# A scan written level by level between the tiles of four projections

## The chip, the cores and the metric

One core of one Trainium2 chip runs the whole kernel in one launch. The metric is the device time of the launch in microseconds (us), as a median over runs. The engines are named as the profile names them: PE is TensorE's matmul side and PEld its weight load, DVE is VectorE, ACT is ScalarE, POOL is GpSimd, SP is SyncE, which here only issues DMAs.

## The reference

One layer of a decoder trunk on 1024 tokens of width 1024, all in float32: a combined input projection, three mixers, an output projection with layer norm, and a mixture of experts. The change touches the input projection and the third mixer, a gated linear recurrence (HGRN2) with 4 heads of 64x64 state:

```
h = x @ w_in                     # 2840 columns, split into gu, gv, nq, ..., hq, hf, hi, hg
def hgrn2_mixer(q, f_logit, i, lower_bound):
    log_f = logaddexp(log(lb), log1p(-lb) + log_sigmoid(f_logit))
    k = (1 - lb) * sigmoid(-f_logit)
    def step(S, inp):            # chunk after chunk, S is the 64x64 state of a head
        b = cumsum(lfc, axis=2)
        decay = exp(where(causal, b[t] - b[s], -inf))
        attn = einsum('bhtd,bhsd,bhtsd->bhts', qc, kc, decay)
        o = attn @ ic + (qc * exp(b)) @ S
        S = exp(b_last) * S + (kc * exp(b_last - b)).T @ ic
    ...
y_a = gmlp_mixer(gelu(gu), gelu(gv), ...)     # first mixer: takes gu and gv
y   = head_rms_norm(concat(y_a, y_b, y_c)) ; y_c part * silu(hg)
```

Here `i` is the column group hi ("the values"), `q` is hq, `f_logit` is hf, and hg is the output gate. hi is needed where `attn` meets `ic`, in its diagonal part, and in the state's update; hg, gv and gu are not needed in the recurrence at all.

## The kernel before

**Stages.** `phase1` loads x, turns it, makes all projections, the recurrence and the gMLP mixer; `phase2` does the attention mixer and the output projection; `moe` the experts. In the profiled run the first stage covers about the first 335 us.

**Projections.** A float32 product is made of three single-pass products of a high and a low part (`mm3`, L78: lines L83, L84, L85 are its three matmuls). `load_w` (L136) fetches 256 columns of w_in in four DMAs on SP (L144), makes the high part on ACT (L72) and the low part on POOL (L76). The weight tiles are two in turn, so a load waits until the projection before the last is through with its tile. `token_major(w, c)` (L199) makes 128 tokens by 256 columns: 24 matmuls into one PSUM tile `pj`. `feature_major` (L149) makes 128 columns by 512 tokens. `pj` has three buffers. "A tile" below is one `token_major` call with the copy that takes its result out of PSUM; hi, hg, gv and gu have eight each (c = 0 to 7), 32 in all.

**The recurrence.** `hgrn` (L489) is called four times, for a pair of heads j and a half hh of the sequence: (0,0), (0,1), (1,0), (1,1). A call has three parts. The front (L499 to L537) makes gates, the running sum b (L510, DVE) and `dgs`, the diagonal of attn; L537, on POOL, starts the result yc as hi times dgs. Then come seven levels (LEVELS = 64 to 1) that build the matrix A by halving: POOL subtracts (L548), ACT takes two exponentials (L549, L550), DVE multiplies three times (L551 into `kq`, L554 twice into `qq`; both double buffered), PE makes 8 matmul records (L557) into `lv`, and DVE copies the level into A under a mask (L558). Last, for four chunks in turn, PE multiplies A by hi (L569) and the state by q (L572), DVE adds to yc (L573), PE makes the state's update (L576) and DVE applies it (L580). A has a single buffer; POOL clears it (L540).

**The order.** The program is not run in the order in which it is written. The compiler (L1596, `schedule_with_timeline_sim=True`) lays out each engine's queue ahead of time on a modelled timeline: of the instructions that are ready there, the one written first goes first. On the chip each queue then keeps that order. Written order is therefore a priority. Before the change it is: features of hf, features of hq, all eight tiles of hi (copied out by DVE, L241), the four calls of `hgrn`, the eight tiles of hg (copied out by ACT, L247), those of gv and gu (ACT, L251), and then the columns of the attention mixer.

Of the kernel before, what the change touches and what calls it, by code (L numbers as in the profile page):

```python
# [10 lines left out]
AF = mybir.ActivationFunctionType  # L11
OP = mybir.AluOpType
# [7 lines left out]
NT = 8  # L20
# [31 lines left out]
class Trunk:  # L52
# [71 lines left out]
    def phase1(self, ctx_nsa, ctx_q, x1d, acc):  # L124
# [60 lines left out]
        with ExitStack() as ctx:  # L185
# [13 lines left out]
            def token_major(w, c):  # L199
                wh, wl, n = w  # L200
                pj = ps.tile([128, 512], F32, name="pj", bufs=3)
                sl = slice(c % 4 * 128, c % 4 * 128 + 128)
                self.mm3(pj[:, :n], KD, lambda k: [xs[c // 4][p][:, k, sl] for p in range(2)], lambda k: [w[p][:, k, 0:n] for p in range(2)])
                return pj
# [19 lines left out]
            with ExitStack() as c2:  # L224
                hp = self.pool(c2, "hgw")
                self.hgrn_consts(hp)
                fl, hq = {}, {}
                for j in range(2):
                    for hh in range(2):
                        pj = feature_major(w, 128 * j, hh)  # L230
                        fl[j, hh] = hp.tile([128, 512], F32, name="fl", bufs=2)
                        nc.scalar.activation(fl[j, hh], pj, AF.Copy)
                w = load_w((C_HQ, 256))
                for j in range(2):
                    for hh in range(2):
                        pj = feature_major(w, 128 * j, hh)
                        hq[j, hh] = hp.tile([128, 512], F32, name="hq", bufs=4)
                        nc.scalar.activation(hq[j, hh], pj, AF.Copy)
                w = load_w((C_HI, 256))
                for c in range(NT):  # L240
                    nc.vector.tensor_copy(hi[:, c], token_major(w, c)[:, :256])  # L241
                for j in range(2):
                    for hh in range(2):
                        self.hgrn(hp, fl[j, hh], hq[j, hh], hi, yc, j, hh)
                w = load_w((C_HG, 256))
                for c in range(NT):
                    nc.scalar.activation(hgt[:, c], token_major(w, c)[:, :256], AF.Copy)  # L247
                for c0, dst in ((C_GV, gv), (C_GU, gu)):
                    w = load_w((c0, 256))
                    for c in range(NT):  # L250
                        nc.scalar.activation(dst[:, c], token_major(w, c)[:, :256], AF.Copy)  # L251

            ns = self.pool(self.ctx, "nsa", side="right")
            self.gate = ns.tile([128, NT, 24], F32, name="gate")
# [231 lines left out]
            nc.gpsimd.memset(t, 0.0)  # L486
        self.nlev = 0

    def hgrn(self, hp, fl, hq, hi, yc, j, hh):  # L489

        nc, ps = self.nc, self.ps
        W = 512
        tmp = lambda: hp.tile([128, W], F32, name="tmp", bufs=4)
        chunk = lambda t: t.rearrange("p (c t) -> p c t", t=128)
        k = hp.tile([128, W], F32, name="k", bufs=2)
        b = hp.tile([128, W], F32, name="b", bufs=2)

        t1, t2, t3 = tmp(), tmp(), tmp()
        nc.scalar.activation(t1, fl, AF.Abs)  # L499
        nc.scalar.activation(t1, t1, AF.Exp, scale=-1.0)  # L500
        nc.scalar.activation(t1, t1, AF.Ln, bias=1.0)
        nc.vector.tensor_scalar(t2, fl, -60.0, None, OP.max)
        nc.scalar.activation(t2, t2, AF.Exp, scale=-1.0)
        nc.scalar.activation(t2, t2, AF.Ln, bias=1.0, scale=self.lb[:, j:j + 1])
        nc.vector.scalar_tensor_tensor(t1, fl, 0.0, t1, OP.min, OP.subtract)
        nc.gpsimd.tensor_tensor(k, t1, fl, OP.subtract)
        nc.scalar.activation(k, k, AF.Exp)
        nc.gpsimd.tensor_scalar(k, k, self.oml[:, j:j + 1], None, OP.mult)
        nc.gpsimd.tensor_tensor(t1, t1, t2, OP.add)
        nc.vector.tensor_tensor_scan(b, self.rs, t1, 0.0, OP.mult, OP.add)  # L510
        bc = chunk(b)

        qe = hp.tile([128, W], F32, name="qe", bufs=2)
        nc.scalar.activation(qe, b, AF.Exp)
        ebl = hp.tile([128, 4], F32, name="ebl", bufs=2)
        nc.vector.tensor_copy(ebl, chunk(qe)[:, :, 127])
        nc.vector.tensor_tensor(qe, qe, hq, OP.mult)
        nc.gpsimd.tensor_tensor(chunk(t3), bc[:, :, 127:128].to_broadcast([128, 4, 128]), bc, OP.subtract)
        nc.scalar.activation(t3, t3, AF.Exp)
        nc.vector.tensor_tensor(t3, t3, k, OP.mult)  # L520
        kt = hp.tile([128, 4, 128], F32, name="kt", bufs=2)
        pt = ps.tile([128, 4, 128], F32, name="lv", bufs=3)
        for u in range(4):
            nc.tensor.transpose(pt[:, u], t3[:, u * 128:(u + 1) * 128], self.ident)
        nc.scalar.activation(kt, pt, AF.Copy)

        t4 = tmp()
        nc.gpsimd.tensor_tensor(t4, hq, k, OP.mult)
        dg = ps.tile([128, 4, 2], F32, name="o", bufs=2)
        for u in range(4):  # L530
            nc.tensor.matmul(dg[:, u], t4[:, u * 128:(u + 1) * 128], self.hs, start=True, stop=True)
        dgs = hp.tile([128, 4, 2], F32, name="dgs", bufs=2)
        nc.vector.tensor_copy(dgs, dg)
        hij = hi[:, 4 * hh:4 * hh + 4, j * 128:(j + 1) * 128]
        ycj = yc[:, 4 * hh:4 * hh + 4, j * 128:(j + 1) * 128]
        heads = lambda t: t.rearrange("p c (e d) -> p c e d", d=64)
        nc.gpsimd.tensor_tensor(heads(ycj), heads(hij), dgs[:, :, :, None].to_broadcast([128, 4, 2, 64]), OP.mult)  # L537

        A = hp.tile([128, 4, 2, 128], F32, name="A", bufs=1)
        nc.gpsimd.memset(A, 0.0)  # L540
        for l, h in enumerate(LEVELS):
            w = 2 * h
            kb, qb = self.kq[self.nlev % 2], self.qq[self.nlev % 2]
            self.nlev += 1
            dd = tmp()
            seg = lambda t: t.rearrange("p (s w) -> p s w", w=w)
            bs, ds, qs, ks, kbs = seg(b), seg(dd), seg(hq), seg(k), seg(kb)
            nc.gpsimd.tensor_tensor(ds, bs, bs[:, :, h - 1:h].to_broadcast([128, W // w, w]), OP.subtract)  # L548
            nc.scalar.activation(ds[:, :, 0:h], ds[:, :, 0:h], AF.Exp, scale=-1.0)  # L549
            nc.scalar.activation(ds[:, :, h:w], ds[:, :, h:w], AF.Exp)  # L550
            nc.vector.tensor_tensor(kbs[:, :, 0:h], ks[:, :, 0:h], ds[:, :, 0:h], OP.mult)  # L551
            for e in range(2):
                r = slice(64 * e, 64 * e + 64)
                nc.vector.tensor_tensor(qb[r, e].rearrange("p c (g h) -> p (c g) h", h=h), qs[r, :, h:w], ds[r, :, h:w], OP.mult)  # L554
            lv = ps.tile([128, 4, 2, 64], F32, name="lv", bufs=3)
            for u in range(4):
                nc.tensor.matmul(lv[:, u], kb[:, u * 128:(u + 1) * 128], qb[:, :, u, :], start=True, stop=True)  # L557
            nc.vector.copy_predicated(  # L558
                A.rearrange("p c e (g two h) -> p (c e) g two h", two=2, h=h)[:, :, :, 1, :],
                self.lmi[:, None, l, :].to_broadcast([128, 8, 64]).rearrange("p u (g h) -> p u g h", h=h),  # L560
                lv.rearrange("p u e (g h) -> p (u e) g h", h=h))

        for u in range(4):
            c = 4 * hh + u
            sl = slice(u * 128, (u + 1) * 128)
            o = ps.tile([128, 128], F32, name="o", bufs=2)
            Sc, Sn = self.S[j][c % 2], self.S[j][(c + 1) % 2]
            for e in range(2):
                nc.tensor.matmul(o[:, e * 64:e * 64 + 64], A[:, u, e, :], hij[:, u, e * 64:e * 64 + 64],  # L569
                                 start=(c == 0 or e == 0), stop=(c == 0))  # L570
            if c:
                nc.tensor.matmul(o, qe[:, sl], Sc, start=False, stop=True)  # L572
            nc.vector.tensor_tensor(ycj[:, u], ycj[:, u], o, OP.add)  # L573
            if c < NT - 1:
                su = ps.tile([128, 128], F32, name="o", bufs=2)
                nc.tensor.matmul(su, kt[:, u], hij[:, u], start=True, stop=True)  # L576
                for e in range(2):
                    r = slice(64 * e, 64 * e + 64)
                    if c:
                        nc.vector.scalar_tensor_tensor(Sn[r, r], Sc[r, r], ebl[r, u:u + 1], su[r, r], OP.mult, OP.add)  # L580
                    else:
                        nc.vector.tensor_copy(Sn[r, r], su[r, r])
# [1017 lines left out]
```

## Time and profile before

| | us |
|---|---|
| median of the runs shown | 1260.39 |
| lowest run | 1260.23 |
| the profiled execution: time | 1260.82 |
| the profiled execution: span of its instructions | 1259.1 |
| PE busy in the span | 1152.3 (92%) |
| DVE busy | 838.4 (67%) |
| ACT busy | 682.1 (54%) |
| POOL busy | 486.7 (39%) |
| mean granted clock of TensorE | 0.963 |

Times in the trace count from the first instruction of the span. The profiled execution takes 1.7 us more than its span, and it lies 0.4 us over the median. A busy share is a mean over stages with different limits, so the rows further down are all cut to a stretch of time: 61.5 to 225 us holds the eight tiles of hi, the scan and the tiles of hg, gv and gu.

### The profile page before, as it was taken

What the parts mean: (1) busy time and instruction counts of PE and PEld (TensorE: products, weight loads), DVE (VectorE), ACT (ScalarE), POOL (GpSimd) and SP (SyncE); (2) the same over time, 40 slices, a digit from 0 to 9 for tenths busy, and PEclk for the clock granted to TensorE, in tenths of its full rate; (3) what the DMA queues carried; (4) which work ended last, traced back from release to release, by engine and by line L of the source; (5) the groups of instructions that cost most, each with busy time, mean ns of one, the idle gap of its engine ahead of it and who ended that gap; (6) DMA issues with size and microseconds to landing.
All of it is one profiled execution on the core that took longest, in us unless ns stands there. A gap on an engine that the chain in (4) does not pass through costs nothing. (4 is left out here: it accounts for less than half of the span.)

```text
span 1259.1 us, 18585 instructions
## 1 busy us (share of the span) xinstructions
PE 1152.3 (92%) x6413; PEld 976.5 (78%) x6413; DVE 838.4 (67%) x1473; ACT 682.1 (54%) x1310; POOL 486.7 (39%) x530
## 2 busy tenths in 40 slices
PE   8998789999897999998898999889999999999992
PEld 6898789888786777787777777668888878888871
DVE  4238876654336778778787876648675875856677
ACT  5416473432436557547474643447575775665672
POOL 6535853563236455433434344112130320311144
PEclk9999899999899999999999899889999999999997
DMA  6120101655135122102111006759887997979782
GB/s 220 42 51 18 34 2 34 178 159 152 49 117 172 38 93 76 68 26 68 42 52 42 35 1 240 250 140 324 309 275 251 302 388 247 329 249 337 240 281 116
DMA packets 92913, 190.41 MB, mean 151 GB/s; under 512 B 15964, under 2 KB 50812, under 8 KB 92784
## 3 DMA queue, kind: packets, MB, share of 16 engines
q1 hardware_dynamic: 81984, 161.97, 38.1%
q0 software_dynamic: 8208, 21.59, 7.5%
q10 hardware_dynamic: 2592, 5.25, 1.1%
q8 instruction: 67, 1.10, 0.4%
q14 instruction: 62, 0.51, 0.1%
HBM read 163.15 MB, written 32.06 MB: 155 GB/s over the span
## 5 line engine op out<-in xcount | busy, mean ns | idle before, releaser
L49 DVE TENSOR_TENSOR wl<-raw,wh 128x1024 fp32r<-128x1024 f32 x192 | 226.5, 1220 | 46.7 <-ACT wh L49 46.4
L49 ACT ACTIVATE wh<-raw 128x1024 fp32r<-128x1024 f32 x192 | 189.7, 1051 | 5.2 <-PE T L49 2.7
L685 POOL TENSOR_SCALAR p<-p,co 128x640 f32<-128x640 f32 (+7 forms) x128 | 89.6, 719 | 97.8 <-DVE co L678 87.2
L727 ACT ACTIVATE p<-S,nm 128x640 f32<-128x640 f32 (+7 forms) x128 | 89.6, 708 | 30.4 <-DVE nm L718 13.7
L72 ACT ACTIVATE th<-T 128x512 fp32r<-128x512 f32 (+1 forms) x148 | 81.4, 580 | 41.0 <-PE T L749 39.1
L76 DVE TENSOR_TENSOR tl<-T,th 128x512 fp32r<-128x512 f32 (+1 forms) x148 | 94.3, 652 | 7.5 <-ACT th L72 6.8
L83 PE MATMUL pj<-wh,xh 128*128 128x256 f32 (+1 forms) x320 | 94.0, 294 | 2.2 <-DVE gate L311 2.2
L84 PE MATMUL pj<-wl,xh 128*128 128x256 f32 (+1 forms) x320 | 94.1, 294 | 0.0
L85 PE MATMUL pj<-wh,xl 128*128 128x256 f32 (+1 forms) x320 | 93.8, 293 | 0.0
L76 POOL TENSOR_TENSOR wl<-wraw,wh 128x512 fp32r<-128x512 f32 (+1 forms) x44 | 61.5, 1410 | 78.9 <-ACT wh L72 78.6
L49 POOL DMA_INDIRECT acc<-yv,idx x21 | 38.9, 1855 | 132.2 <-ACT yv L49 122.8
L49 PE MATMUL u<-wh,xth 128*128 128x256 f32 (+1 forms) x256 | 86.9, 340 | 0.0
L749 PE MATMUL T<-ident,p 128*128 128x128 f32 x528 | 85.4, 287 | 1.0 <-DVE ks L168 1.0
L718 DVE TENSOR_REDUCE nm<-S 128x1 f32<-128x640 f32 (+7 forms) x96 | 85.1, 886 | 1.5
L49 PE MATMUL u<-wh,xtl 128*128 128x256 f32 (+1 forms) x256 | 84.9, 332 | 0.0
L49 PE MATMUL u<-wl,xth 128*128 128x256 f32 (+1 forms) x256 | 84.8, 331 | 0.0
L752 PE MATMUL O<-tl,v 128*128 128x512 f32 x132 | 63.1, 478 | 19.0 <-DVE tl L76 18.3
L49 PE MATMUL y<-wh,hth 128*128 128x512 f32 x184 | 76.6, 416 | 4.2 <-ACT hth L49 3.5
L712 PE MATMUL S<-ks,q 128*128 128x512 f32 (+3 forms) x192 | 70.1, 368 | 11.0 <-ACT pc L696 7.7
L749 PEld LDWEIGHTS T<-ident,p 128*128 128x128 f32 x528 | 69.1, 149 | 13.1 <-issue 2.5
L49 PE MATMUL g<-wh,xth 128*128 128x512 f32 x184 | 74.5, 405 | 1.7 <-ACT xth L49 1.7
L49 PE MATMUL g<-wh,xtl 128*128 128x512 f32 x184 | 74.5, 405 | 0.0
(411 smaller groups left out, 3210.0 us busy)
## 6 DMA issues: line engine op xcount, KB each, us to landing
raw<-in_exp_w_gate_dram SPq DMA_DIRECT2D x64, 512.0 KB, 4.5
raw<-in_exp_w_up_dram SPq DMA_DIRECT2D x64, 512.0 KB, 8.6
raw<-in_exp_w_down_dram SPq DMA_DIRECT2D x64, 512.0 KB, 10.3
wraw<-in_w_in_dram SPq DMA_DIRECT2D x36, 256.0 KB, 2.7
q<-qd SPq DMA_DIRECT2D x64, 128.0 KB, 3.9
xr<-in_x_dram SPq DMA_DIRECT2D x8, 512.0 KB
x<-in_x_dram SPq DMA_DIRECT2D x8, 512.0 KB, 4.1
raw<-acc SPq DMA_DIRECT2D x8, 512.0 KB, 7.6
```

The source lines that it names most:

```text
L49: return lambda *a, **k: self.tc.keep_in_program_order(getattr(self.engine, name)(*a, **k))
L72: A.activation(hi, src, AF.Copy)
L76: (G if eng == "g" else V).tensor_tensor(lo, src, f(hi), OP.subtract)
L83: nc.tensor.matmul(ps, lh, rh, start=(k == 0), stop=False)
L84: nc.tensor.matmul(ps, lh, rl, start=False, stop=False)
L85: nc.tensor.matmul(ps, ll, rh, start=False, stop=(k == n - 1))
L685: nc.gpsimd.tensor_scalar(P[b][h], P[b][h], co[:, b, h:h + 1], 0.0, OP.mult, OP.add)
L712: nc.tensor.matmul(reg, hd(0, h0 + u), ks, start=True, stop=False)
L718: nc.vector.tensor_reduce(nm[:, 1 + br, h0:h0 + per], S.rearrange("p (u k) -> p u k", u=per)[:, :, 0:n], axis=AX, op=OP.max, negate=True)
L727: nc.scalar.activation(P[1 + br][h], S[:, 512 * u:512 * u + n], AF.Exp, bias=nm[:, 1 + br, h:h + 1], accum_out=sums[:, 1 + br, h:h + 1])
L749: nc.tensor.transpose(Tp[:, h], P[b][h][:, kb * 128:kb * 128 + 128], self.ident)
L752: nc.tensor.matmul(O, v, t, start=(n == 0 and t is th), stop=(n == len(jobs) - 1 and t is tl))
```

## The change

Three things. The four projections hi, hg, gv and gu become one generator, `projections`, that yields after each tile; all 32 results are copied out by ACT, where hi's eight were copied out by DVE. `hgrn` takes one tile after each level, and in the call (0,0) one more behind the seventh level, so that all of hi is written before A first meets it: 8 + 7 + 7 + 7 tiles, and the last three of gu behind the scan. Since `load_w` stands inside the generator, a weight load is written where the first tile of its projection is asked for. And L537 (yc = hi times dgs, POOL) moves from ahead of the levels to behind them. No tile, buffer or matmul is added or removed.

```diff
-                w = load_w((C_HI, 256))
-                for c in range(NT):
-                    nc.vector.tensor_copy(hi[:, c], token_major(w, c)[:, :256])
+
+                def projections():
+
+                    for c0, dst in ((C_HI, hi), (C_HG, hgt), (C_GV, gv), (C_GU, gu)):
+                        w = load_w((c0, 256))
+                        for c in range(NT):
+                            nc.scalar.activation(dst[:, c], token_major(w, c)[:, :256], AF.Copy)
+                            yield
+
+                beside = projections()
                 for j in range(2):
                     for hh in range(2):
-                        self.hgrn(hp, fl[j, hh], hq[j, hh], hi, yc, j, hh)
-                w = load_w((C_HG, 256))
-                for c in range(NT):
-                    nc.scalar.activation(hgt[:, c], token_major(w, c)[:, :256], AF.Copy)
-                for c0, dst in ((C_GV, gv), (C_GU, gu)):
-                    w = load_w((c0, 256))
-                    for c in range(NT):
-                        nc.scalar.activation(dst[:, c], token_major(w, c)[:, :256], AF.Copy)
+                        self.hgrn(hp, fl[j, hh], hq[j, hh], hi, yc, j, hh, beside)
+                for _ in beside:
+                    pass
...
-        hij = hi[:, 4 * hh:4 * hh + 4, j * 128:(j + 1) * 128]
-        ycj = yc[:, 4 * hh:4 * hh + 4, j * 128:(j + 1) * 128]
-        heads = lambda t: t.rearrange("p c (e d) -> p c e d", d=64)
-        nc.gpsimd.tensor_tensor(heads(ycj), heads(hij), dgs[:, :, :, None].to_broadcast([128, 4, 2, 64]), OP.mult)
...
                 lv.rearrange("p u e (g h) -> p (u e) g h", h=h))
+            next(beside, None)
+        if j == hh == 0:
+            next(beside)
+        hij = hi[:, 4 * hh:4 * hh + 4, j * 128:(j + 1) * 128]
+        ycj = yc[:, 4 * hh:4 * hh + 4, j * 128:(j + 1) * 128]
+        heads = lambda t: t.rearrange("p c (e d) -> p c e d", d=64)
+        nc.gpsimd.tensor_tensor(heads(ycj), heads(hij), dgs[:, :, :, None].to_broadcast([128, 4, 2, 64]), OP.mult)
```

## Rows read from the trace of the kernel before

**Rows 1.** Stretches: us, length, busy (x) of five engines, granted clock, DMA share.
```profile
61.50:85.80 24.30, 24.30 (x207) 24.25 (x206) 3.07 (x8) 4.21 (x9) 6.15 (x5) 1.00 0.17 45
85.80:225.00 139.20, 122.11 (x955) 118.59 (x956) 105.59 (x172) 75.59 (x133) 76.44 (x58) 0.94 0.09 24
```

**Rows 2.** PE's waits, 55 to 230 us: who waited for whom, total, times, longest.
```profile
PE lv L557 <- DVE qq L554: 6.9, 7, 2.3
PE o L569 <- DVE A L558: 6.3, 3, 2.5
PE o L569 <- DVE yc L573: 3.0, 1, 3.0
```

**Rows 3.** DVE's timeline: start, length, line, operation, [idle before <- releaser].
```profile
71.50 0.42 DVE L241 COPY hi<-pj 128x256 f32<-128x256 f32 x1 [2.41 <-PE pj L85]
74.35 0.43 DVE L241 COPY hi<-pj 128x256 f32<-128x256 f32 x1 [2.42 <-PE pj L85]
...
134.41 2.30 DVE L510 TENSOR_TENSOR_SCAN b<-rs,tmp 128x512 f32<-128x512 f32 x1 [1.94 <-POOL tmp L509]
136.63 2.68 DVE L558 COPY_PREDICATED A<-lmi,lv 128x512 f32<-128x512 int32 x2
```

**Rows 4.** PE's timeline: matmuls of the scan, with and without a wait.
```profile
91.20 1.13 PE L557 MATMUL lv<-qq,kq 128*128 128x128 f32 x8 [0.20 <-DVE qq L554]
...
175.63 1.13 PE L557 MATMUL lv<-qq,kq 128*128 128x128 f32 x8 [1.02 <-DVE qq L554]
...
191.83 1.16 PE L557 MATMUL lv<-qq,kq 128*128 128x128 f32 x8 [2.29 <-DVE qq L554]
...
208.68 1.05 PE L557 MATMUL lv<-qq,kq 128*128 128x128 f32 x8
...
214.47 0.55 PE L569 MATMUL o<-hi,A 128*128 128x64 f32 x4
```

**Rows 5.** Groups of DVE's instructions, 61.5 to 225 us: busy, mean ns, idle before.
```profile
L554 DVE TENSOR_TENSOR qq<-hq,tmp 64x256 f32<-64x256 f32 x52 | 36.2, 696 | 0.5
...
L551 DVE TENSOR_TENSOR kq<-k,tmp 128x256 f32<-128x256 f32 x26 | 20.9, 805 | 4.3 <-ACT tmp L549 4.0
```

**Rows 6.** Groups of POOL's and ACT's instructions, 61.5 to 225 us, as rows 5.
```profile
L76 POOL TENSOR_TENSOR wl<-wraw,wh 128x512 fp32r<-128x512 f32 x16 | 22.8, 1442 | 9.3 <-ACT wh L72 9.3
L537 POOL TENSOR_TENSOR yc<-hi,dgs 128x512 f32<-128x512 f32 x4 | 4.4, 1090 | 1.9 <-DVE dgs L533 1.9
...
L549 ACT ACTIVATE tmp<-tmp 128x256 f32<-128x256 f32 x24 | 10.1, 422 | 11.1 <-POOL tmp L548 11.0
L247 ACT ACTIVATE hgt<-pj 128x256 f32<-128x256 f32 x8 | 2.9, 367 | 0.0
```

**Rows 7.** Timelines of POOL, DVE and PE at 142 to 149 us, as rows 3.
```profile
142.46 4.99 POOL L268 TENSOR_TENSOR hgt<-hgt,gain 128x2048 f32<-128x2048 f32 x1
142.97 4.76 DVE L551 TENSOR_TENSOR kq<-k,tmp 128x256 f32<-128x256 f32 x1
147.98 0.66 PE L569 MATMUL o<-hi,A 128*128 128x64 f32 x4 [2.97 <-DVE yc L573]
```

**Rows 8.** Stretches with a low granted clock, columns as rows 1.
```profile
136.00:150.00 14.00, 7.94 (x50) 7.27 (x49) 13.64 (x12) 7.42 (x13) 14.00 (x8) 0.86 0.16 39
150.00:158.00 8.00, 6.79 (x30) 6.50 (x31) 4.70 (x9) 0.00 (x0) 3.75 (x4) 0.50 0.24 64
...
183.00:188.00 5.00, 4.91 (x30) 4.74 (x29) 3.50 (x8) 3.23 (x8) 4.12 (x4) 0.66 0.02 5
```

**Rows 9.** ACT's timeline: when a weight load could start; a copy that waited long.
```profile
61.64 1.15 ACT L72 ACTIVATE wh<-wraw 128x512 fp32r<-128x512 f32 x2 [1.28 <-PE pj L84]
...
158.17 0.38 ACT L251 ACTIVATE gv<-pj 128x256 f32<-128x256 f32 x1 [13.72 <-PE pj L85]
```

**Rows 10.** PE's waits behind the first stage, 333 to 1259 us, as rows 2.
```profile
PE O L752 <- DVE tl L76: 18.3, 18, 3.1
PE T L49 <- DVE sg L49: 8.8, 15, 1.8
```

More of the change, by code (lines that the diff above doesn't have):

```diff
@@ L487, in hgrn_consts, with hgrn @@
         self.nlev = 0
-    def hgrn(self, hp, fl, hq, hi, yc, j, hh):
+    def hgrn(self, hp, fl, hq, hi, yc, j, hh, beside):
         nc, ps = self.nc, self.ps
```

## The prediction, made before the changed kernel was run

> **What bounds the stage now.** I read first the stretches of time, cut where the eight tiles of hi end, then PE's waits inside them, then the timelines of PE and DVE at those waits, and last the groups of instructions on DVE, POOL and ACT. Two things are to be seen in the stretches [rows 1]. From 61.5 to 85.8 us PE is busy all of 24.3 us, while DVE has 3.1 us of work, ACT 4.2 and POOL 6.2: the tiles of hi run alone and the scan stands still beside them, because they are written ahead of it. From 85.8 to 225 us, 139.2 us, PE is busy 122.1 us, so 17.1 us of it are idle, and the granted clock is 0.94 in the mean. DVE is then busy 105.6 us, 76%: the scan is squeezed into the second stretch, and PE waits for it. The tiles of hg, gv and gu already run between its levels there, although they are written behind it: the idle time of PE has nearly the length of its waits for DVE (16.2 us in three groups, [rows 2]), and none of these is for a projection. So what the change can give is not overlap as such, which the compiler has made, but a better order.
>
> PE's waits name the pieces [rows 2]: 6.9 us before the levels' matmuls (L557), 6.3 us before the first product with A in three of the four calls, 3.0 us once for yc.
>
> **A ceiling.** PE's work is the same after. Its pieces with a low clock are 14 us at 0.86, 8 us at 0.50 and 5 us at 0.66 [rows 8]; brought to full clock they would be shorter by 14 x 0.14 + 8 x 0.50 + 5 x 0.34 = 2.0 + 4.0 + 1.7 = 7.7 us. Each of them lies behind one of the waits of 2 to 3 us. All waits and all of the clock together are 17.1 + 7.7 = 24.8 us, a little too much, since some waits lie in the slow pieces. That is the most that this stage can give: 1260.8 - 24.8 = 1236.0 against the profiled execution's own 1260.8 us.
>
> **The change part by part.**
>
> *The levels' waits, 6.9 us in seven places.* A tile takes 2.85 us of PE (the copies of hi end at that distance, 71.50 and 74.35, [rows 3]). Before, a level's matmuls are written ahead of every tile of hg, gv and gu, so the compiler puts them into PE's queue the moment that it believes DVE done, and any lateness of DVE shows. I counted the projection matmuls between a level and the work of the scan before it. Ten of the 28 levels have 14 or more; they run from 91.20 to 208.68 and two of them wait, 0.20 and 1.02 us [rows 4], 0.12 us each in the mean. The other five waits, 5.7 us together, stand behind seven or fewer; 2.29 us at 191.83 is one with none [rows 4]. After, a tile of 24 matmuls is written between any two levels and has the higher priority. I take 0.12 us for each of 28 levels, 3.4 us left, a gain of 3.5 us. Bounds: 0 (the queue comes out as before) and 6.9.
>
> *The first product with A, 6.3 us in three places.* These already stand behind 27 or 28 projection matmuls, so a tile ahead of them is no cure by itself. The timeline of DVE shows what was late [rows 3]: the running sum of the next call (L510), which waited 1.94 us for POOL, stood ahead of the last masked copies into A. In the fourth call no next one follows, and there is no wait (214.47, [rows 4]). After, the levels are held to the pace of the tiles and the front of the next call is not, so it should meet the middle of the levels more often than their end. Half, 3.1 us; bounds 0 and 6.3.
>
> *The wait for yc, 3.0 us.* POOL's multiplication of the gate (L268, 4.99 us) ran, and a multiplication of DVE that takes 0.81 us in the mean [rows 5] took 4.76 us beside it; PE waited 2.97 us behind that [rows 7]. L268 stays and comes at another place: half, 1.5 us; bounds 0 and 3.0.
>
> *The clock, 7.7 us.* The slow pieces follow the waits, and I keep about half of those: half, 3.9 us; bounds 0 and 7.7.
>
> *L537 behind the levels.* POOL, 1.09 us each [rows 6]; it waits for dgs and hi, which are there by then, and behind it in POOL's queue stand the next call's subtractions. DVE's first addition to yc needs it. In three calls the next call's work covers it; in the last one at most its length shows. Cost 1.1 us; bounds 0 and 4.4.
>
> *The copies of hi.* DVE loses eight of 0.42 us [rows 3], in a stretch where it was idle, and ACT gains eight of 0.37 us (as those of hg, [rows 6]): 2.9 us, hidden by ACT's idle time (75.6 of 139.2 us busy, [rows 1]); with the cover gone, 2.9 us.
>
> *The weight loads.* All four stand at other places in the text. Each is four DMAs on SP, four copies on ACT and four subtractions on POOL of 1.44 us [rows 6]. A load is let go by its buffer and not by its place: the one at 61.64 waited for PE [rows 9]. I cost it at nothing, since the one for hi has the features of hq ahead of it on PE, and the one for hg the tiles of hi. What changes is company: subtractions that ran beside an idle DVE now run beside levels, 6.2 us of POOL's work in the first stretch [rows 1], which is the bound; the tile between two levels (2.85 us) hides them one by one.
>
> **The sum.** 3.5 + 3.1 + 1.5 + 3.9 - 1.1 = 10.9 us, of 24.8 at most. The profiled execution goes from 1260.8 to 1249.9; it lies 0.4 us over the median, so the median is forecast at 1249.5 us. Behind the stage nothing is edited and PE is busy 92% of the whole span, so I expect the gain to arrive whole. But the compiler lays out everything again: the largest waits there are 18.3 and 8.8 us [rows 10], and a third of these, either way, is 9 us, which I put into the range.
>
> **The rivals.**
>
> *The waits stay: 1260.8.* The scan has the same DVE and POOL work, and these hold each other up: a multiplication into kq takes 0.81 us in the mean [rows 5], yet one beside a long instruction of POOL took 4.76 [rows 7]. If PE's lateness comes from that and not from the order, the waits keep their sum over the longer stretch and only move. For it: the work beside DVE grows in the first stretch. Against it: DVE's 108.7 us in both stretches fall to 105.3, which is 69% of the 152.6 us that would be left after a gain of 10.9, and no longer 76% as in the second stretch. The time is 1260.8, give or take 4. The Trainium skill has a rule for this: page "SBUF — State Buffer", section "Who interferes with whom", says that a VectorE instruction with two SBUF inputs and a GpSimd instruction that reads SBUF lock each other out for a whole instruction, so that running the scan beside the weight splits buys less than the busy shares say. By that rule alone the sum would be the rival's. The trace agrees with the rule (4.76 us inside a POOL instruction of 4.99), and whether order or lock sets the sum no row of before tells.
>
> *Slower: ACT's queue, 1276.* All evictions now stand in ACT's queue between the exponentials of the levels. One of gv already waited 13.72 us for its tile [rows 9], and everything behind it waited too. If each of 28 levels had its exponentials behind a copy that waits half a tile, 1.42 us, the scan would be 40 us longer; it starts 24.3 us earlier, so the end moves by 40 - 24.3 = 15.5 us, to 1276. It decides from 24.3 / 28 = 0.87 us a level. Against it: the eight copies of hg between levels waited 0.0 us, and the exponentials' waits are for POOL (11.0 of 11.1 us) [rows 6].
>
> *All of it: 1236.* The ceiling, if the tile between two levels covers every lateness of DVE. For it: ten levels behind 14 matmuls or more wait only 0.12 us each. Against it: the waits for A, which have 27 matmuls ahead of them.
>
> **How the numbers follow.** Forecast (1240 to 1256): 0.61. Waits stay: 0.19. Slower by ACT's queue: 0.10. All of it: 0.10. The range that leaves out no more than 2 in 10 runs from the ceiling to past the rival without gain: 1237 to 1263; the likeliest case alone has 1240 to 1256. About 2% (25 us) is what a measurement of this kernel can tell from no change. Faster by more needs under 1235.2, the whole ceiling and something behind the stage: 0.07. Slower by more needs over 1285.6, the third rival at more than its price: 0.05. Within 2%: 0.88.
>
> **What would show it.** Right: from 61.5 to 85.8 us DVE busy around 17 us (69% of 24.3) and not 3; the first call's product with A near 92 us (61.5 + 8 tiles of 2.85 + 7 levels of 1.05, [rows 4]); PE's wait for the levels under 4 us; the last addition to yc about 11 us earlier than before; granted clock over the stretch near 0.97. Wrong: PE's waits for DVE again 16 us in sum though the first stretch is mixed (the first rival); ACT waiting for `pj` with its exponentials queued behind, at many levels (the second); or a gain in the stage that is lost again behind 333 us.

## The result and the profile after

The changed kernel takes 1240.57 us in the median (1238.01 to 1241.9 over four runs), the kernel before 1260.23 beside it: a ratio of 0.9849, with a 95% interval of 0.9824 to 0.9873. Two executions, one of the kernel before (1835.3 us) and one of e2 further down (1787.5 us, at a mean granted clock of 0.67), were of a slower state and count in no median or ratio here. The gain is 19.7 us (16 to 22 by the interval), where the forecast was 10.9 (1249.5, range 1237 to 1263). The time lies in the range and the sign is right; the size is nearly twice the forecast, and the likeliest case (1240 to 1256) holds it by 0.6 us only. The gain is 1.5%, so it lies within the 2% that the forecast gave 0.88 to; the interval excludes a ratio of 1 all the same. The profiled execution after took 1241.9 us with a span of 1240.1, so it is to be held against the span of 1259.1 before.

First the stretches, cut at the same places of the work in both: the end of the last tile of gu on PE, the first score of the attention mixer, a place in the middle behind it, the end. Columns are as in [rows 1]. Of after:

```profile
61.50:85.80 24.30, 24.30 (x209) 24.16 (x208) 17.17 (x26) 16.66 (x29) 14.36 (x12) 1.00 0.17 45
61.50:207.20 145.70, 137.23 (x1164) 135.71 (x1163) 103.42 (x173) 79.13 (x146) 80.78 (x67) 1.00 0.11 30
207.20:311.90 104.70, 101.83 (x541) 88.81 (x541) 58.10 (x78) 37.52 (x82) 53.63 (x56) 1.00 0.60 162
311.90:714.00 402.10, 366.20 (x2038) 301.55 (x2037) 298.81 (x697) 234.16 (x634) 177.14 (x223) 0.96 0.21 65
714.00:1240.10 526.10, 480.20 (x2420) 395.99 (x2419) 353.38 (x482) 299.38 (x401) 129.65 (x119) 0.96 0.77 256
```

The same work in the kernel before:

```profile
61.50:224.20 162.70, 145.61 (x1157) 142.22 (x1156) 108.66 (x179) 79.00 (x139) 82.59 (x63) 0.95 0.11 27
224.20:333.60 109.40, 105.58 (x548) 92.28 (x547) 56.45 (x79) 38.62 (x83) 55.42 (x60) 0.97 0.57 155
333.60:733.00 399.40, 364.43 (x2028) 299.97 (x2027) 297.04 (x693) 233.46 (x632) 177.13 (x222) 0.96 0.21 65
733.00:1259.10 526.10, 480.83 (x2430) 396.57 (x2429) 354.47 (x487) 300.34 (x404) 132.95 (x119) 0.96 0.77 256
```

The stage of the change gives 162.7 - 145.7 = 17.0 us. The stretch behind it, where no line was edited, gives 4.7 more. The third gives 2.7 back, and the last is the same. The 2.7 is no more than profiled executions differ by: from the first attention score to the end, the profiled runs below need from 925.2 to 931.2 us (before 925.5, after 928.2) and none of their edits lies there. In the first 24.3 us DVE is busy 17.2 us where it was 3.1 [rows 1]: the scan runs beside the tiles of hi.

PE's waits from 61.5 us to the last tile of gu, after (columns as in [rows 2]), and behind the "..." the one line of waits from there to the first score:

```profile
PE lv L555 <- DVE qq L552: 3.1, 2, 1.8
PE o L574 <- DVE A L556: 2.5, 3, 1.5
PE lv L526 <- DVE tmp L522: 2.0, 1, 2.0
PE o L574 <- DVE yc L578: 0.9, 1, 0.9
...
PE o L408 <- DVE pws L407: 2.9, 2, 2.3
```

Against [rows 2] the three groups went from 6.9, 6.3 and 3.0 us to 3.1, 2.5 and 0.9, and a new one of 2.0 came, before the transposes at the head of a call (L526). From the last tile of gu to the first score the kernel before has two waits, and a stretch of low clock behind each:

```profile
PE pj L83 <- DVE gate L311: 2.2, 1, 2.2
PE o L406 <- DVE cbias L407: 1.6, 1, 1.6
```

```profile
260.00:268.00 8.00, 6.48 (x24) 5.54 (x25) 5.51 (x7) 5.19 (x14) 6.67 (x5) 0.79 0.67 181
304.00:312.00 8.00, 6.65 (x40) 6.68 (x41) 2.53 (x9) 0.39 (x1) 2.93 (x15) 0.79 0.84 225
```

PE's timeline after shows the order that was written for the first call, eight matmul records of a level, then the 24 of a tile (left out here), then the first product with A; and in the second call the two waits before a level, each right behind the 24 matmuls of a tile:

```profile
63.16 1.14 PE L555 MATMUL lv<-qq,kq 128*128 128x128 f32 x8
...
66.97 1.05 PE L555 MATMUL lv<-qq,kq 128*128 128x128 f32 x8
...
93.13 0.66 PE L574 MATMUL o<-hi,A 128*128 128x64 f32 x4 [0.75 <-DVE A L556]
...
118.57 1.13 PE L555 MATMUL lv<-qq,kq 128*128 128x128 f32 x8 [1.77 <-DVE qq L552]
...
123.85 1.13 PE L555 MATMUL lv<-qq,kq 128*128 128x128 f32 x8 [1.29 <-DVE qq L552]
```

One more table, worked out from the stretches, serves for all runs. From 61.5 us to the first attention score I cut the trace into slices of 2 us and sum three things: PE's idle time; the time lost to the clock (PE's busy time in a slice times one minus its granted clock); and the rest, which is PE's work at full clock.

| kernel | first score at | PE idle | lost to the clock | rest |
|---|---|---|---|---|
| before | 333.6 | 20.9 | 11.0 | 240.2 |
| after | 311.9 | 11.3 | 0.0 | 239.1 |
| e1, hi behind the levels, no turns | 322.6 | 16.2 | 5.7 | 239.1 |
| e3, turns in the first call only | 320.4 | 14.9 | 5.3 | 238.6 |
| e7, every other level in the later calls | 322.0 | 16.2 | 5.6 | 238.7 |
| e2b, hi whole in front, then turns | 333.9 | 26.8 | 7.0 | 238.5 |
| e4, yc ahead of the levels | 315.2 | 11.8 | 1.7 | 240.2 |
| e5, hi copied by DVE | 316.4 | 10.2 | 6.2 | 238.5 |
| e6 and e6b, gate in eight (one kernel) | 311.2, 312.3 | 10.3, 9.8 | 0.0, 1.7 | 239.4, 239.3 |
| e8, e1 with the gate in eight | 319.8 | 14.0 | 4.5 | 239.8 |
| e9, before with the gate in eight | 325.8 | 17.0 | 7.5 | 239.9 |
| e12, a second gate multiplication | 314.1 | 9.0 | 4.7 | 238.9 |

The rest stays between 238.5 and 240.2 us in thirteen executions, so the stage's time is PE's work plus idle plus lost clock, and the gain of 21.7 us up to the first score is 9.6 of idle, 11.0 of clock and 1.1 of rest.

### The profile page after: what moved, and what is told of

Its sections match the earlier page's. It is cut to its first block, busy times and chain, and to the rows that moved or that the text cites. A ratio compares the mean times of both kernels' runs of the same rounds, so it can differ in the third digit from the quotient of the medians.

```text
span 1240.1 us, 18581 instructions
## 1 busy us (share of the span) xinstructions
PE 1140.5 (92%) x6413; PEld 967.0 (78%) x6413; DVE 834.9 (67%) x1465; ACT 680.7 (55%) x1315; POOL 479.8 (39%) x530
## 5 line engine op out<-in xcount | busy, mean ns | idle before, releaser
L85 PE MATMUL pj<-wh,xl 128*128 128x256 f32 (+1 forms) x320 | 91.1, 285 | 0.0
L84 PE MATMUL pj<-wl,xh 128*128 128x256 f32 (+1 forms) x320 | 91.0, 284 | 0.0
```

The lines of the kernel that those rows point to most:

```text
L84: nc.tensor.matmul(ps, lh, rl, start=False, stop=False)
L85: nc.tensor.matmul(ps, ll, rh, start=False, stop=(k == n - 1))
```

## The experiments

The theories to be told apart: the *start* (the scan begins 24 us earlier, and that alone is the gain), the *order* (a tile between any two levels keeps PE's lateness from showing), the *lock* (DVE is late because of POOL's long instructions, whatever the order), and what two side edits cost (L537's new place, hi's copies on ACT). Ratios are to the kernel before, measured in the same job, with 95% intervals. Diffs are against the changed kernel unless they say otherwise.

### e1: early start without turns

All eight tiles of hi are written behind the seven levels of the first call, and all others behind the scan.

```diff
-            next(beside, None)
         if j == hh == 0:
-            next(beside)
+            for _ in range(NT):
+                next(beside)
```

> No turns at all: all eight tiles of hi are written in one piece behind the seven levels of the first call, those of hg, gv and gu behind the scan as before; copies by ACT and yc's start behind the levels as in the changed kernel. Theory T1 (a tile written between two levels keeps PE from coming to the levels too early, and that is most of the gain): the scan starts early, but PE's waits for DVE from 61.5 us to the end of the scan come back to 12 us or more (before 16.8, changed 8.5), clock pieces below full speed come back, and the time lies between 1248 and 1260. Theory T2 (it is enough that the scan no longer waits for the whole of hi): 1238 to 1244, waits as in the changed kernel. Theory T3 (DVE and POOL hold each other up and set the waits, whatever the order): waits as before, about 1258 to 1262.

Measured: 1250.8 us, 0.9947 (0.9919 to 0.9974), as T1 had it: PE's waits for DVE up to the scan's end are 12.7 us again. The early start alone gives about 7 to 9 us, under half of the gain. Two stretches of its trace, one around its longest wait and one from the scan's end to the last tile of gu:

```profile
158.00:168.00 10.00, 7.09 (x43) 7.13 (x44) 6.90 (x14) 2.04 (x6) 7.01 (x6) 0.66 0.20 56
...
200.80:215.80 15.00, 15.00 (x128) 14.86 (x126) 12.69 (x17) 4.88 (x8) 6.91 (x4) 1.00 0.75 196
```

The scan ends at 200.8 us, 5.7 earlier than in the changed kernel (its last addition to yc starts at 206.5), and 15 us of projections run alone behind it: matmuls that could have stood in PE's waits in the scan. The longest of these waits is 5.29 us, and its cause is seen on three engines:

```profile
151.19 5.58 POOL L270 TENSOR_TENSOR hgt<-hgt,gain 128x2048 f32<-128x2048 f32 x1 [0.33 <-ACT hgt L269]
...
153.36 3.44 DVE L518 COPY ebl<-qe 128x4 f32<-128x4 f32 x1 [0.96 <-ACT qe L516]
...
160.91 1.09 PE L574 MATMUL o<-hi,A 128*128 128x64 f32 x4 [5.29 <-DVE A L556]
```

A copy of four columns takes 3.44 us and ends at 156.80, where POOL's multiplication of the gate ends (151.19 + 5.58 = 156.77); the two masked copies into A stand behind it on DVE, and PE behind those.

### e3 and e7: turns in the first call only, and half of the turns

e3 keeps the turns in the call (0,0) and writes the tiles of hg, gv and gu behind the scan. e7 gives the three later calls a tile at every other level.

```diff
-            next(beside, None)
+            if j == hh == 0:
+                next(beside)
```

> Turns in the first call alone, with hi; hg, gv and gu written behind the scan as before. T1: the first call ends near 92 us as in the changed kernel, and the waits of calls two to four come back (10 us or more of the 13 that they had before), with slow clock behind them: 1247 to 1256. T2: 1238 to 1244 as changed.

```diff
-            next(beside, None)
+            if j == hh == 0 or l % 2:
+                next(beside, None)
```

> Half the dose: the first call as in the changed kernel, in the other three calls a tile of hg, gv or gu only behind every second level (nine tiles), the remaining 15 behind the scan. T1 (slack per level): between e3 (1251.6) and the changed kernel (1240.6), 1243 to 1249, with slow clock pieces in the stage. T2' (turns matter only for hi, and what e3 lost is chance): 1250 to 1253 as e3. T2'' (any turns in the later calls suffice): 1239 to 1242.

Measured: e3 1251.61 us, 0.9927 (0.9900 to 0.9954), in T1's range; e7 1250.92 us, 0.9928 (0.9908 to 0.9947), not between e3 and the changed kernel, as T1 had it. Neither differs from e1 beyond the intervals. Turns for hi alone add nothing to the early start, and half of the later turns add nothing either; the second half brings the rest, some 10 us. The waits of e7, over 61 to 335 us:

```profile
PE o L575 <- DVE A L556: 6.3, 3, 5.3
...
PE lv L555 <- DVE qq L552: 2.6, 3, 1.0
```

The levels' wait is 2.6 us, less than the 3.1 of the changed kernel (in e3 1.0, in e1 3.4). So a tile between any two levels is not needed to bring the levels' waits down; the early start alone does as much. What stays without all of the turns is the wait for A, with its piece of 5.3 us beside the gate, and the clock that is lost behind it.

### e2: turns without the early start

The eight tiles of hi are written whole in front of the scan again; the other 24 are written by turns.

```diff
+                for _ in range(NT):
+                    next(beside)
                 for j in range(2):
...
-        if j == hh == 0:
-            next(beside)
```

> The other half alone: hi stays whole in front of the scan, and the 24 tiles of hg, gv and gu are written one behind each level from the first call on (none is left for the last four levels). T1: the levels' waits (L557 before) fall under 3 us though the scan starts as late as before; the stretch of hi stays idle on DVE, so the scan's end moves less; 1248 to 1256. T2: no gain, 1257 to 1263, since the start is what counts. T3: no gain either, waits about 16 us.

> e2 once more for a profile at the usual clock (its own was taken in a disturbed execution). As e2: hi whole in front, then turns. From its timed runs (1266.2 us, no gain): the scan ends at 230 us or later, more than 20 us behind the last tile of gu, and PE idles between the two in the stretch that follows, 20 us or more in all up to the first attention score, where the kernel before has 20.9.

Measured: e2 1265.23 us, 1.0036 (0.9999 to 1.0073): no gain, over the range of T2 even. The lines are of e2b, the same kernel in a single execution (1260.93 us). Of its forecast, the scan's end (228.3 us) came sooner than the 230 given, and PE's idle time up to the first score (26.8 us, the table) is over the 20. Its stretches, cut at the last tile of gu (204.1) and the last addition to yc (228.3):

```profile
85.80:204.10 118.30, 108.33 (x904) 106.84 (x904) 93.77 (x152) 77.93 (x134) 74.15 (x58) 0.99 0.11 28
204.10:228.30 24.20, 24.00 (x134) 20.39 (x133) 11.36 (x20) 5.99 (x9) 7.01 (x7) 1.00 0.18 47
228.30:333.90 105.60, 88.94 (x469) 79.03 (x470) 55.85 (x79) 33.50 (x76) 49.56 (x54) 0.92 0.55 150
```

And its two largest waits of PE, 61 to 335 us:

```profile
PE pj L83 <- DVE gate L315: 10.6, 1, 10.6
...
PE pj L83 <- ACT fx L392: 4.0, 2, 3.3
```

Inside the turns the clock is 0.99, as the order would have it, and PE waits 1.7 us for the levels, under the 3 of T1. But 24 tiles are used up 24 us before the scan ends, the later columns are taken forward to fill in, and then PE waits 10.6 and 4.0 us in the next stretch for their consumers, at a clock of 0.92. The gain is moved and given back. In the changed kernel tiles and scan end together, at 207.2 and 206.5 us. That alone is not enough: in the kernel before they did so too (224.2 and 226.0 us), behind 24 us in which the scan stood still.

### e4: yc started ahead of the levels in the later calls

L537's line (now L566) goes back ahead of the levels wherever hi is already there, in three calls of four.

```diff
+        diagonal = lambda: nc.gpsimd.tensor_tensor(heads(ycj), heads(hij), dgs[:, :, :, None].to_broadcast([128, 4, 2, 64]), OP.mult)
+        if j or hh:
+            diagonal()
...
-        nc.gpsimd.tensor_tensor(heads(ycj), heads(hij), dgs[:, :, :, None].to_broadcast([128, 4, 2, 64]), OP.mult)
+        if j == hh == 0:
+            diagonal()
```

> The changed kernel with yc's start (hi times dgs, POOL) put back ahead of the levels in the last three calls; in the first call it stays behind them, since hi is not written before. My prediction charged its new place with 1.1 us: if that was right, the time falls by about 1 us against the changed kernel; if the place costs nothing, no difference (within 1.5 us).

Measured: 1240.88 us, 0.9837 (0.9816 to 0.9857), the same as the changed kernel. No cost of L537's place is to be seen.

### e5: hi copied by DVE

```diff
-                            nc.scalar.activation(dst[:, c], token_major(w, c)[:, :256], AF.Copy)
+                            if dst is hi:
+                                nc.vector.tensor_copy(dst[:, c], token_major(w, c)[:, :256])
+                            else:
+                                nc.scalar.activation(dst[:, c], token_major(w, c)[:, :256], AF.Copy)
```

> The changed kernel with hi's eight tiles copied out by DVE again (8 times 0.42 us) and not by ACT. Theory T1: DVE is what PE waits for, but the first call has a tile between any two levels, so no more than 1.5 us slower. If ACT's queue were what costs (the prediction's rival of ACT), it would be faster by 1 us or more.

Measured: 1244.36 us, 0.9874 (0.9857 to 0.9891); beside e4 of the same job it is 3.5 us longer, and the intervals only touch; that of the changed kernel (0.9824 to 0.9873) overlaps. So a loss is likely, more than the 1.5 us expected, but not shown beyond the noise. In the trace one of the eight copies stands ahead of a level's products, and PE is late where it was not. Timelines of DVE and PE:

```profile
82.73 0.40 DVE L246 COPY hi<-pj 128x256 f32<-128x256 f32 x1
...
84.21 1.30 DVE L552 TENSOR_TENSOR kq<-k,tmp 128x256 f32<-128x256 f32 x1
85.43 2.66 DVE L555 TENSOR_TENSOR qq<-hq,tmp 64x256 f32<-64x256 f32 x2
...
88.24 1.81 PE L558 MATMUL lv<-qq,kq 128*128 128x128 f32 x8 [2.06 <-DVE qq L555]
```

The same products in the changed kernel:

```profile
83.42 0.41 DVE L549 TENSOR_TENSOR kq<-k,tmp 128x256 f32<-128x256 f32 x1
83.75 0.85 DVE L552 TENSOR_TENSOR qq<-hq,tmp 64x256 f32<-64x256 f32 x2
```

They start 0.8 us later in e5, and then take 3.88 us from start to end in place of 1.18: multiplications of POOL run beside them without a gap (84.18 to 87.81 us). By these rows it is less the length of the copy than what the products then run beside. The stretch around that wait:

```profile
86.00:94.00 8.00, 5.94 (x38) 5.79 (x37) 7.89 (x10) 1.45 (x4) 4.69 (x5) 0.79 0.01 2
```

That level did not wait in the changed kernel. The idle sum of e5 (10.2 us) is no larger than that of after, though; its whole loss in the table is clock, 6.2 us in four pieces, each behind a wait of 2.1 to 2.4 us. Only the first piece, 1.5 us, lies beside the tiles of hi; waits at the places of the other three are found in the changed kernel too, where the clock did not fall.

### e6, e8, e9 and e12: POOL's long instruction

The gate's multiplication (L268, now L270) in eight pieces of 256 columns: e6 in the changed kernel (e6b is the same kernel again), e8 in e1, e9 in the kernel before. e12 does a second multiplication of the same size, by ones; e11, which was to do it by a maximum, has no result.

```diff
-            nc.gpsimd.tensor_tensor(hgt, hgt, gain[:, None, 256:512].to_broadcast([128, NT, 256]), OP.mult)
+            for c in range(NT):
+                nc.gpsimd.tensor_tensor(hgt[:, c], hgt[:, c], gain[:, 256:512], OP.mult)
```

> The changed kernel with POOL's multiplication of the output gate (4.58 us, one instruction) cut into eight of 256 columns. If the long POOL instruction is what makes DVE late at 141 to 163 us (the new wait of 2.0 us before the transposes and part of the waits behind it), those waits go and the time falls by 1 to 3 us against the changed kernel (1238 to 1240); if it only moves work that PE has cover for, nothing changes (within 1.5 us).

> The changed kernel with the gate's multiplication in eight pieces once more, in more rounds. If the one wait of 2.0 us beside POOL's long instruction is worth its length, 1238 to 1239 us, a ratio to before of 0.983; if the order absorbs it, 1240.6 and 0.985.

> e1 (no turns) with POOL's gate multiplication cut into eight. In e1 one wait of 5.3 us before the first product with A, and slow clock behind it, lies beside that instruction (5.58 us on POOL, in which a DVE copy of four elements took 3.44 us). Theory T4 (that one instruction, not the lack of turns, is what e1 loses against the changed kernel): 1239 to 1244. T1 (turns): the wait goes, 2 to 4 us are won, and the rest of the loss stays: 1246 to 1249.

> The kernel before, with POOL's gate multiplication (4.99 us) cut into eight. There PE waited 2.97 us for yc beside it, and the stretch from 150 to 158 us behind that had half the clock (4 us lost). Theory T4 (that one long instruction makes DVE late, and the clock follows): the wait for yc goes, and 4 to 8 us are won, 1252 to 1256. Theory T1 (the order alone): no more than the 1.5 us that half of the wait is worth, 1258 to 1260.

```diff
+            unit = gw.tile([128, 1], F32, name="unit")
+            nc.gpsimd.memset(unit, 1.0)
+            nc.gpsimd.tensor_tensor(hgt, hgt, unit[:, :, None].to_broadcast([128, NT, 256]), OP.mult)
```

> The changed kernel with POOL's long multiplication of the gate (4.6 us) done a second time, by ones. If it is POOL's long instruction that holds up DVE and so PE behind the gate, this doubles it: one more wait of PE of 2 to 5 us for DVE in the first stage, and, should the clock fall behind that wait, 1243 to 1249 us. If the tiles between the levels cover it, 1239 to 1242, as the changed kernel (1240.6).

Measured: e9 1254.03 us, 0.9935 (0.9909 to 0.9961): the kernel before gains 6 to 8 us by this edit alone (by the medians and by the ratio), as T4 had it, and its wait of 3.0 us for yc [rows 2] is gone. e8 1248.54 us, 0.9903 (0.9884 to 0.9922), beside e1's 0.9947, is T1's number: the wait of 5.29 us is 1.3 in PE's waits, the rest of the loss stays, and in DVE's timeline the same copy is no longer held:

```profile
PE o L575 <- DVE A L557: 1.6, 2, 1.3
```

```profile
153.54 0.29 DVE L519 COPY ebl<-qe 128x4 f32<-128x4 f32 x1 [0.96 <-ACT qe L517]
```

e6 1238.24 us, 0.9834 (0.9803 to 0.9865), and e6b 1239.63 us, 0.9834 (0.9810 to 0.9858): the lowest medians of the study, 0.9 to 2.3 us under the changed kernel's, but the intervals overlap its own, so it is not shown to be better. The new wait before the transposes does fall from 2.0 to 0.2 us, and those of the levels rise from 3.1 to 4.1; in e6, over 61.5 to 207.1 us:

```profile
PE lv L556 <- DVE qq L553: 4.1, 3, 2.1
...
PE lv L527 <- DVE tmp L523: 0.2, 1, 0.2
```

e12 1242.58 us, 0.9852 (0.9819 to 0.9884): this tells nothing, since the second multiplication (3.60 us) was laid at 193.2 us, into a time when DVE stood waiting for PE anyway.

Taken together, the gate in eight parts the change from the lock, as far as it does nothing else. With it the kernel before has 0.9935 (e9), the early start 0.9903 (e8), early start and turns 0.9834 (e6): the change is then worth some 13 us (4 for the start, 9 for the turns) and not 19, so the turns do not gain by the lock alone. The other 6 us would be what the changed order saves by keeping PE out of the lock's way; the intervals of the four ratios are nearly as wide as that, so it is an estimate from them and not shown.

Where the lock does not reach PE is to be seen in the changed kernel's own timeline, beside the gate:

```profile
140.95 4.58 POOL L270 TENSOR_TENSOR hgt<-hgt,gain 128x2048 f32<-128x2048 f32 x1
...
142.84 2.97 DVE L549 TENSOR_TENSOR kq<-k,tmp 128x256 f32<-128x256 f32 x1 [0.68 <-PE lv L555]
...
142.49 0.36 PE L83 MATMUL pj<-wh,xh 128*128 128x256 f32 x1
```

DVE is held here too (2.97 us, where a kq takes 0.78 in the mean), but at that moment PE has 67 projection matmuls in its queue, from 142.49 to 150.68 us, and doesn't wait.

## Why the prediction was right, and where it was short

*The mechanism held.* The bound was read rightly: the tiles of hi ran alone, PE's idle time was its waits for DVE, and an earlier start and a better order took about half of them away. The first product with A came at 93.13 us (forecast near 92), DVE was busy 17.17 us in the first stretch (around 17), and the levels' wait was 3.1 us (under 4). Two signs were missed: the last addition to yc came 19.5 us earlier (226.0 to 206.5), not 11, and the clock was 1.00, not 0.97.

*Term by term*, the gain in us:

| term | forecast | measured |
|---|---|---|
| levels' waits, 6.9 | 3.5 | 3.8 |
| first product with A, 6.3 | 3.1 | 3.8 |
| wait for yc, 3.0 | 1.5 | 2.1 |
| new wait before L526 | none | -2.0 |
| clock, 61.5 us to the last tile of gu | 3.9 | 7.6 |
| L537 behind the levels | -1.1 | 0 |
| the stretch behind it | none | 4.7 |

The rows measured add up to 20.0 us; small waits (0.9) and PE's own work (0.8) make it 21.7 up to the first score. The waits were sized well, 7.7 us in the net against 8.1, though the reason given for the levels is not borne out: the early start without all of the turns (e1, e3, e7) leaves 1.0 to 3.4 us of them too, as turns without the early start leave 1.7 (e2b), and in the changed kernel both waits that are left (1.77 and 1.29 us) stand right behind the 24 matmuls of a tile, where 0.12 us a level was forecast. That 3.1 us came where 3.4 was forecast to be left is luck. *The clock* was the term that failed. "I keep about half of those: half" kept half of the slow pieces because half of the waits were kept; half of PE's idle time was kept (17.1 to 8.5 us), and yet in this execution no slow piece was left. *The step "nothing is edited behind the stage"* failed next: the two slow pieces and a wait of the following stretch went as well (another grew from 1.6 to 2.9 us), 4.7 us in all, and the forecast had no term for them. *L537* was charged 1.1 us, and no cost is to be seen (e4). *The weight loads* were costed at nothing, and no wait of PE stands behind them, though ACT now waited 8.0 us for their DMAs and only 1.0 before. *The copies of hi* were costed at nothing on the ground that DVE had been idle in that stretch; in the changed kernel it no longer is, and there the move to ACT is worth perhaps 3.5 us (e5). The cover was read from the kernel before, at a place that the change itself fills.

*Early start or order?* About half each in the profiled executions, where by the times the start has 7 to 9 of 19.7 us. The start alone (e1) takes 4.7 us of idle and 5.3 of clock, the turns on top of it 4.9 and 5.7 (the table above). Turns alone give nothing (e2).

*The rivals.* "The waits stay" fell, though its mechanism is real: beside POOL's long instruction one of DVE's takes 2.97 to 4.76 us in every kernel that has it whole, it makes most of the wait of 5.3 us in e1 (1.3 in e8) and stands ahead of the same wait in e3 and e7, and freed of it the kernel before gains 6 to 8 us. It did not keep the sum of the waits, and part of the gain may be that the changed order puts tiles beside it (some 6 us, the estimate above). The page "SBUF — State Buffer" of the Trainium skill, section "Who interferes with whom", says that such a lock lasts for a whole instruction and names plain copies among what can take it; the trace agrees (the copy of four columns in e1, 3.44 us, ended with POOL's instruction). The sum of that rule alone, no gain, did not come. "ACT's queue" fell: the rows of ACT, 61 to 207 us, after, show that the exponentials waited for POOL alone, and that a copy waited for long only at the end, in gu (from 184 us on), with no exponential of a level behind it:

```profile
L547 ACT ACTIVATE tmp<-tmp 128x256 f32<-128x256 f32 x24 | 10.2, 424 | 26.9 <-POOL tmp L546 26.9
L245 ACT ACTIVATE hi<-pj 128x256 f32<-128x256 f32 x8 | 2.9, 365 | 0.0
L245 ACT ACTIVATE gu<-pj 128x256 f32<-128x256 f32 x7 | 2.7, 384 | 18.0 <-PE pj L85 18.0
```

"All of it" (1236) was half true: in the stage 17.0 us of the ceiling of 24.8 came, all of the clock and about half of the waits. The forecast's fear for the time behind 333 us was not borne out: what came back there, 2.7 us, is no more than executions differ by.

*What stays open.* How much of the clock's 11.0 us is due to the change and how much to the one execution that was profiled. Kernels with all turns and hi on ACT (after, e4, e6, e6b, e12) lost 0.0, 1.7, 0.0, 1.7 and 4.7 us in theirs, those without all of it 4.5 to 7.5, before 11.0: the direction holds, the zero does not. Up to the last tile of gu, though, four of these five lost nothing (e12 1.7), so what is left to chance lies mostly in the stretch behind. Filling PE's waits with matmuls that compute nothing, which would separate clock from idle, was not tried. Why half of the turns give nothing was seen (the wait of 5.3 us stays) but not taken apart further: e7 was not run with the gate in eight. That the front of the next call meets the middle of the levels more often, the reason given for the waits for A, was not tested.

## What to carry to other kernels

Where a dependent chain and independent matmuls share PE, start the chain early and spread all of the independent work over the whole of it, so that both end together: too early a use (e2) leaves PE waiting behind the chain's end, too late a one (e1) lets it run alone. Cost short waits at their length and add something for the clock: here 9.6 us less of idle time came with 11.0 us less of lost clock, and over the thirteen executions the lost clock was between nothing and 0.6 of the idle time. And read the cover of a moved instruction where it will stand after the change, not where it stood.

## What was not expected of the hardware

The clock after a short wait is not fixed by the program. e6 and e6b are the same kernel; PE's wait in front of the same matmul (L409) was 2.38 us in one and 2.35 in the other, and then the granted clock over the same 8 us was 1.00 and 0.79. PE's timeline of e6 and that stretch of it:

```profile
241.13 0.38 PE L409 MATMUL o<-one,pws 128*128 128x1 f32 x2 [2.38 <-DVE pws L408]
```

```profile
240.00:248.00 8.00, 6.33 (x28) 5.00 (x29) 5.48 (x6) 3.85 (x11) 6.22 (x4) 1.00 0.54 140
```

The same two of e6b:

```profile
241.49 0.42 PE L409 MATMUL o<-one,pws 128*128 128x1 f32 x2 [2.35 <-DVE pws L408]
```

```profile
240.00:248.00 8.00, 6.51 (x23) 5.33 (x24) 5.49 (x6) 4.21 (x12) 6.45 (x4) 0.79 0.59 155
```

The two ran on different chips; but the six executions of e1, all on one chip, have mean clocks from 0.962 to 0.972 and times from 1256.48 to 1249.08 us. So a wait of this size is a chance of a loss, here of some 1.7 us, and a single profile's clock should not be read as the kernel's. The other surprise was how little DVE work a lock needs: a copy that takes 0.29 us beside the short pieces (e8) held up DVE for 3.44 us beside the long one (e1), and PE waited 5.29 us behind it in place of 1.31.
